# Keys and queries of an attention projected together, 512 columns at a time

## The chip, the cores and the metric

The kernel runs on one core of a Trainium2 chip. The metric is the device time of one execution in microseconds (us): the median of three runs of the kernel before is 1073.49 us (1072.52 to 1073.66). Five engines work side by side, each through its own instructions in a fixed order: TensorE (PE) multiplies matrices, and its weight loads are listed apart as PEld; VectorE (DVE), ScalarE (ACT) and GpSimd (POOL) work elementwise; SyncE (SP) only issues DMA transfers. ACT and POOL issue DMA transfers too.

## The reference

One layer of a hybrid decoder over 512 tokens with 16 meta tokens ahead of them: a first feed-forward network, a token-mixing part with two attention branches, and a second feed-forward network. The part that matters here is the mixing. Cut to it:

```
h   = rms_norm(x, g)
qkv = h @ w_in                       # 1024 inputs
fox: 8 heads of 64, q k v; log_f = log_sigmoid(h @ w_f + b)   # one forget value per token and head
     s = (rms(q) . rms(k)) / 8 + c[q] - c[k],  c = cumsum(log_f); causal softmax; times v
swa: 8 query heads, 2 key/value heads of 64, window 128, sinks, relative bias; softmax; times v
two gated branches, summed and projected
```

Each query and key head is normalised over its 64 values before the scores. Everything is float32 in and out.

## The kernel before

Every float32 product is made of three matmuls of a rounded format: both operands are split into a high and a low part, and high x high, high x low and low x high are summed in PSUM. Weights arrive by DMA as pieces of up to 128 x 1024 (raw, three buffers, issued by SP at line 252), ACT rounds them to wh (L133), and DVE subtracts to wl (L140). The helper piece() hands out the next split piece and keeps loads and splits a few pieces ahead.

Mixing is projected in chunks of 256 columns: for fox, two halves of four heads each with a chunk for v, k and q; for the sliding branch one of k and v and two of q. A chunk takes two pieces, each of four of the eight blocks of inputs, and goes over the tokens in tiles: tile 0 is the meta tokens, 16 rows, multiplied by a packed copy xm (two matmuls a block, tok_step at L1005 and L1006), then four tiles of 128 tokens with 24 matmuls of 256 columns each (prod, L301 to L304). tok_chunk makes two half-steps for each tile. After a tile of keys or queries, head_norm runs: ACT squares (L1057), DVE reduces per head (L1058) and scales (L1059), POOL raises to the power -1/2 (L351, rsq), ACT makes a scaled copy (L1072), DVE multiplies by the norm (L1079); the multiply is placed one tile later. When the last tile is through, finish transposes the heads on PE (L1159, L1167), ACT and DVE store the high and low parts (L134, L142).

The forget values become a table of biases. forget_sums transposes them on PE (L1195, L1197), copies and sums them along the tokens on DVE (L1201 to L1204), reorders them on POOL (L1207, L1208) and writes them to memory as cbd by SP (L1205, L1209). load_cb(p) reads them back, spread over all partitions, into a tile cb and a part of zA (L1235): by SP for the first pair of heads, by ACT for the next ones. mask_late(p) puts the causal mask in with an affine select on POOL (L1239). The scores of a pair need kH, kL, qH and, once they leave PSUM, cb.

Attention itself is written as units for each pair of heads, and while a unit's softmax runs, PE is given half-steps of later chunks as fills: a function weave mixes the two lists. Written order is not final: a scheduler with its own costs sets each engine's order when the kernel is built, and each engine then works through its list without overtaking, so that an instruction that waits holds all behind it on the same engine.

oA (the attention outputs) and zA (gates, and in part the biases) live in two tiles of a pool that stays through the mixing and the second feed-forward network. They are empty, but for the biases, while the first chunks are projected. The start of the mixing in code:

```
ka = qk_chunk(f0, "k", every, 1)
qa = qk_chunk(f0, "q", toks, 0)
va = v_chunk(f1)
run(ka[:-1] + qa[:LAG] + ka[-1:] + [forget_sums, lambda: load_cb(0)] + qa[LAG:-1]
    + va[:3] + [lambda: mask_late(0)] + qa[-1:] + va[3:5])
```

## Time and profile before

| | |
|---|---|
| median of three runs | 1073.49 us (1072.52 to 1073.66) |
| the profiled execution | 1073.59 us, span 1071.5 us, TensorE clock 0.999 |
| PE, PEld busy | 1060.0 us, 1028.2 us |
| DVE, ACT, POOL busy | 892.4 us, 664.7 us, 212.3 us |
| the mixing's projections and attention | about 361 to 607 us of the span |

The profile's page gives busy time by engine and the costliest groups of instructions. Other views of the same trace list waits (engine, output and line of the waiting instruction, what released it, total us, times, longest), groups of instructions by line and shape (count, busy us, mean ns of one, idle time before them and what ended it), and a timeline (start in us, duration in us, engine, line, operation, count of merged instructions, and in brackets idle time before it). Matmuls overlap, so the distance from one start to the next is what a matmul costs, not the duration.

### The profile page before, as it was taken

Reading aid. Unit: us, or ns where it says so; the run is one execution under the profiler, and the core shown is the slowest. Engines: PE = TensorE matmul, PEld = TensorE weight load, DVE = VectorE, ACT = ScalarE, POOL = GpSimd, SP = SyncE. Lnnn points to the kernel's source line nnn. Section 1 sums busy time; section 2 is a strip of 40 time slices with the busy share of each in tenths; the row PEclk is TensorE's granted clock in tenths of the full one; section 3 lists DMA queues with packets and bytes.
Section 4 is the critical chain, followed back from the end, with each engine's and each line's share of the span. In section 5 each row is a group of like instructions: output and inputs, shape, how many; then the busy total and the mean of one; then the engine's idle time right before and its main releaser. Section 6 shows DMA issues by size and latency. Waiting matters only on the chain.

```text
span 1071.5 us, 22307 instructions
## 1 busy us (share of the span) xinstructions
PE 1060.0 (99%) x8515; PEld 1028.2 (96%) x8515; DVE 892.4 (83%) x1732; ACT 664.7 (62%) x1270; POOL 212.3 (20%) x281
## 2 busy tenths in 40 slices
PE   9999999999999999999999999999999999999997
PEld 8999999999999999999877899999999999999997
DVE  7988878888889678889887999788988788977884
ACT  7667456656666466667757766455665466645663
POOL 3011111111124442332200110001122111221210
PEclk9999999999999999999999999999999999999999
DMA  8787777688776413313211873657688777887763
GB/s 279 198 224 162 189 193 196 152 216 219 176 180 178 124 65 123 87 52 89 73 59 57 241 196 99 210 184 213 155 203 196 181 185 194 180 179 196 163 123 90
DMA packets 112571, 173.58 MB, mean 162 GB/s; under 512 B 10880, under 2 KB 59264, under 8 KB 112208
## 3 DMA queue, kind: packets, MB, share of 16 engines
q1 hardware_dynamic: 74464, 122.72, 36.5%
q0 software_dynamic: 29040, 37.83, 22.9%
q10 hardware_dynamic: 8960, 11.60, 3.2%
q8 instruction: 67, 1.10, 0.4%
q14 instruction: 40, 0.33, 0.1%
HBM read 167.89 MB, written 6.32 MB: 163 GB/s over the span
## 4 chain that ended last, share of the span: by engine, by line
PE 50%; DVE 2%; ACT 1%; issue 0%; ACTq 0%; DVEq 0%
PE ps L301 9%; PE ps L304 8%; PE ps L302 8%; PE pt L301 8%; PE pt L302 7%; PE pt L304 7%; PE ps L1481 1%; DVE wl L140 0%; PE pt L1481 0%; PE ps L1960 0%; DVE pL L140 0%; ACT t L1216 0%; PE pt L1498 0%; ACT wh L133 0%; PE pt L1500 0%
## 5 line engine op out<-in xcount | busy, mean ns | idle before, releaser
L301 PE MATMUL ps<-x,wh 128*128 128x256 f32 (+2 forms) x768 | 219.8, 286 | 0.2
L302 PE MATMUL ps<-x,wh 128*128 128x256 f32 (+2 forms) x768 | 218.9, 285 | 0.5 <-DVE x L142 0.4
L304 PE MATMUL ps<-x,wl 128*128 128x256 f32 (+2 forms) x768 | 218.8, 285 | 0.0
L140 DVE TENSOR_TENSOR wl<-raw,wh 128x1024 fp32r<-128x1024 f32 (+3 forms) x125 | 150.1, 1201 | 38.4 <-ACT wh L133 37.5
L133 ACT CAST wh<-raw 128x1024 fp32r<-128x1024 f32 (+3 forms) x125 | 128.6, 1030 | 81.3 <-PE ps L302 46.7
L301 PEld LDWEIGHTS ps<-x,wh 128*128 128x128 f32 x768 | 144.7, 189 | 1.8 <-ACT hT L686 0.3
L302 PEld LDWEIGHTS ps<-x,wh 128*128 128x128 f32 x768 | 144.4, 188 | 1.4 <-DVE x L142 0.9
L304 PEld LDWEIGHTS ps<-x,wl 128*128 128x128 f32 x768 | 144.6, 188 | 0.9
L301 PE MATMUL pt<-x,wh 128*128 128x256 f32 (+2 forms) x424 | 125.3, 296 | 0.0
L304 PE MATMUL pt<-x,wl 128*128 128x256 f32 (+2 forms) x424 | 124.6, 294 | 0.0
L133 ACT CAST wh<-tc 128x1024 fp32r<-128x1024 f32 (+1 forms) x70 | 71.8, 1026 | 66.0 <-DVE tc L234 55.7
L302 PE MATMUL pt<-x,wh 128*128 128x256 f32 (+2 forms) x392 | 112.5, 287 | 0.0
L140 DVE TENSOR_TENSOR wl<-tc,wh 128x1024 fp32r<-128x1024 f32 (+1 forms) x70 | 83.5, 1192 | 33.4 <-ACT wh L133 33.2
L301 PE MATMUL ps<-acts,wh 128*128 128x264 f32 (+1 forms) x352 | 100.5, 286 | 0.1
L304 PE MATMUL ps<-acts,wl 128*128 128x264 f32 (+1 forms) x352 | 99.8, 284 | 0.0
L302 PE MATMUL ps<-acts,wh 128*128 128x264 f32 (+1 forms) x352 | 99.7, 283 | 0.0
L140 DVE TENSOR_TENSOR wl<-rawC,wh 128x1024 fp32r<-128x1024 f32 (+1 forms) x70 | 84.2, 1202 | 5.7 <-ACT wh L133 5.2
L133 ACT CAST wh<-rawC 128x1024 fp32r<-128x1024 f32 (+1 forms) x70 | 71.5, 1022 | 22.5 <-PE pt L302 16.6
L301 PEld LDWEIGHTS pt<-x,wh 128*128 128x128 f32 x424 | 80.0, 189 | 2.3 <-ACT wh L133 0.2
L304 PEld LDWEIGHTS pt<-x,wl 128*128 128x128 f32 x424 | 79.8, 188 | 2.1
L302 PEld LDWEIGHTS pt<-x,wh 128*128 128x128 f32 x392 | 73.7, 188 | 0.6
L301 PEld LDWEIGHTS ps<-acts,wh 128*128 128x128 f32 x352 | 66.4, 189 | 0.7 <-DVE h2T L918 0.3
(447 smaller groups left out, 3248.2 us busy)
## 6 DMA issues: line engine op xcount, KB each, us to landing
rawC<-in_w1i_dram SPq DMA_DIRECT2D x20, 512.0 KB, 4.5
raw<-in_w1i_dram SPq DMA_DIRECT2D x40, 256.0 KB, 4.5
raw<-in_w2i_dram SPq DMA_DIRECT2D x40, 256.0 KB, 3.4
rawC<-in_w2i_dram SPq DMA_DIRECT2D x20, 512.0 KB, 4.2
raw<-in_wm_dram SPq DMA_DIRECT2D x18, 512.0 KB, 4.2
raw<-in_wout_dram SPq DMA_DIRECT2D x16, 512.0 KB, 4.3
rawD<-in_w1i_dram SPq DMA_DIRECT2D x20, 256.0 KB, 4.6
raw<-in_w1i_dram POOLq DMA_DIRECT2D x20, 256.0 KB, 5.7
```

Of the source, the lines that this page charges most:

```text
L133: return A.copy(o, i)
L140: return V.tensor_tensor(out=o, in0=i, in1=h, op=ALU.subtract)
L301: PE.matmul(ps, sH, mH, start=first, stop=False, **more)
L302: PE.matmul(ps, sH, mL, start=False, stop=False, **more)
L304: shared["mm"] = PE.matmul(ps, sL, mH, start=False, stop=last, **more)
L1481: PE.transpose(ps[:, P * hh : P * hh + P], ts_[hh][:, c0 : c0 + P], ident)
```

## The change

The chunks of k and q of one fox half become one chunk of 512 columns (kq_chunk), and so do v and k of the sliding branch with the first four of its query heads (kvq_chunk). Such a chunk has four pieces of weights, each of two blocks of inputs by 512 columns, and all four stay until its last tile. The buffers wh and wl hold three pieces beside what the next chunk takes, so the first two pieces of a joined chunk go into home tiles: the places of the first half of zA and the second half of oA. For that, oA and zA (and the later tenants of their places) become two tiles each, behind a class Split. The meta tile is still projected 256 columns wide, since only keys (and values) need it.

The norms of the eight (or six) heads of a joined tile are made together: one square into sqacc, one reduce, one scalar step and one power of eight columns. Scaled queries wait for their transposes in the second half of zA. Finishing is cut into three steps: the keys of the first pair, its queries, and the second pair later, or in the sliding chunk the first key head, all queries, and the second key head. forget_sums and load_cb(0) come after thirteen of the joined chunk's eighteen steps. The later loads of h2T are cut to fit the split tile.

```diff
-    for c in (4, 2, 0, 5, 3, 1, 8, 6, 7):
-        for k in (0, 4):
-            pieces.append(("w", [(wm[c][:, k : k + 4, :], 4, 256)]))
...
+    for cuts in (((4, whole),), ((2, whole), (0, whole)), ((5, whole),), ((3, whole), (1, whole)), ((8, vals), (8, keys_), (6, whole)), ((7, whole),)):
+        nk = 4 if len(cuts) == 1 else 2
+        for k in range(0, KD, nk):
+            part = [(wm[c][:, k : k + nk, w], nk, w.stop - w.start) for c, w in cuts]
...
+            pieces.append(("w", part, k // 2 if nk == 2 and k < 4 else None))
...
+            elif pieces[c][0] == "w" and len(pieces[c]) > 2 and pieces[c][2] is not None:
+                home = kp.tile([P, 2, 1024], F32R, tag=("z0", "o1")[pieces[c][2]], name=nm("home"))
+                wh, wl = home[:, 0], home[:, 1]
...
-    oA = kp.tile([P, 2, 4, S], F32, tag="o", name="oA")
-    zA = kp.tile([P, KD, S], F32, tag="z", name="zA")
+    oA = Split("oA", ("o0", "o1"), [4, S])
+    zA = Split("zA", ("z0", "z1"), [4, S])
+    zA.get(1)
...
+    def wide_chunk(alloc, evac, ends):
+
+        w, box = [None] * 4, {}
+
+        def one(i, j):
+            if i == 0 and j == 0:
+                alloc()
+            if j == 0:
+                box[i] = psum()
+            width = 512 if i else 256
+            for q in (j,) if i else (2 * j, 2 * j + 1):
+                if i == 0:
+                    w[q] = piece()
+                for k in (2 * q, 2 * q + 1):
+                    tok_step(box[i], i, w, k, width)
+            if j == (3 if i else 1):
+                box[i] = evac(i, tok_result(box[i], i, width))
+                if i:
+                    box[i - 1]()
+
+        def end(f):
+            if box[NB] is not None:
+                box[NB]()
+                box[NB] = None
+            f()
+
+        return [lambda i=i, j=j: one(i, j) for i in range(NB + 1) for j in range(4 if i else 2)], [lambda f=f: end(f) for f in ends]
...
-        sq = new("hsq", [P, 256], F32, 3)
-        ss = mp.tile([P, 4], F32, tag="hss", name=nm("hss"), bufs=4)[:n, :nh]
+        sq = new("hsq", [P, 256], F32, 3) if nh <= 4 else sqacc
+        ss = mp.tile([P, 8], F32, tag="hss", name=nm("hss"), bufs=4)[:n, :nh]
...
+    def in_z(j):
+        return zA[:, 4 + (j - 1) // 2, 256 * ((j - 1) % 2) : 256 * ((j - 1) % 2) + 256].rearrange("p (h d) -> p h d", d=HD)
...
+    def kq_chunk(box):
+        ka, ko, kf = heads(box, "k", 1)
+        qa, qo, qf = heads(box, "q", 0, in_z)
...
+        def evac(i, ps):
+            if i == 0:
+                return head_norm(ps, 0, 4, ko(0))
+            return head_norm(ps, i, 8, [(o, par, 0, 4) for o, par in ko(i)] + [(qo(i)[0], None, 4, 8)])
+
+        return wide_chunk(alloc, evac, (lambda: kf([0]), lambda: qf([0]), lambda: [kf([1]), qf([1])]))
...
-    ka = qk_chunk(f0, "k", every, 1)
-    qa = qk_chunk(f0, "q", toks, 0)
+    kq0, ends0 = kq_chunk(f0)
     va = v_chunk(f1)
-    run(ka[:-1] + qa[:LAG] + ka[-1:] + [forget_sums, lambda: load_cb(0)] + qa[LAG:-1] + va[:3] + [lambda: mask_late(0)] + qa[-1:] + va[3:5])
+    run(kq0[:13] + [forget_sums, lambda: load_cb(0)] + kq0[13:] + va[:3] + ends0[:1] + va[3:4] + [lambda: mask_late(0)] + ends0[1:2] + va[4:5])
...
-        va[5:] + k1[:-1] + q1[:LAG] + k1[-1:] + q1[LAG:-1] + kv[:LAG] + q1[-1:],
-        kv[LAG:-1] + qb0[:LAG] + kv[-1:] + qb0[LAG:-1] + qb1[:2] + qb0[-1:] + qb1[2:4],
-        qb1[4:-1] + gates[:LAG] + qb1[-1:] + gates[LAG:],
+        va[5:7] + ends0[2:] + va[7:] + kq1 + kvq[:2] + ends1[:1] + kvq[2:LAG] + ends1[1:2],
+        kvq[LAG : LAG + 1] + ends1[2:] + kvq[LAG + 1 :] + qb1[:1] + ends2[:1] + qb1[1:2] + ends2[1:2] + qb1[2:4],
+        qb1[4:5] + ends2[2:] + qb1[5:-1] + gates[:LAG] + qb1[-1:] + gates[LAG:],
```

How the built order moves at three places. The first is POOL around the end of the first keys and queries, before the change. hss is a tile's norms, t the forget sums, cb and zA the bias tiles. In brackets is what an instruction waits for: DMAHW is the landing of a transfer.

```order
L1289 MEMSET t_5558 128x16 [waits DVE_49,PE_49]
L1207 COPY t_5343<-t_5343 8x128 [waits DVE_49]
L1207 COPY t_5343<-t_5343 8x128 x3
L1208 COPY t_5343<-t_5343 8x16
L351 TENSOR_TENSOR hss_5373<-hss_5373,nhalf 128x4 [waits DVE_49,Pool_49]
L351 TENSOR_TENSOR hss_5407<-hss_5407,nhalf 128x4 [waits DVE_49,Pool_49]
L1289 MEMSET t_5559 128x16 [waits DMAHW7_49,DMAHW0_49,Pool_49]
L1145 MEMSET qn_5815 128x256
L351 TENSOR_TENSOR hss_5441<-hss_5441,nhalf 128x4 [waits DVE_49]
L1239 AFFINE_SELECT zA<-zA 128x2x128 [waits DMAHW1_49]
L1239 AFFINE_SELECT cb_5356<-cb_5356 128x2x128 [waits DMAHW2_49]
```

And in the changed kernel (its L357 is the power, L1325 the select):

```order
L1375 MEMSET t_5415 128x16 [waits DVE_49,PE_49]
L1293 COPY t_5227<-t_5227 8x128 [waits DVE_49]
L1293 COPY t_5227<-t_5227 8x128 x3
L1294 COPY t_5227<-t_5227 8x16
L357 TENSOR_TENSOR hss_5249<-hss_5249,nhalf 128x8 [waits DVE_49]
L1375 MEMSET t_5416 128x16 [waits DMAHW6_49,DMAHW5_49,Pool_49]
L1325 AFFINE_SELECT zA_4880<-zA_4880 128x2x128 [waits DMAHW0_49]
L1325 AFFINE_SELECT cb_5240<-cb_5240 128x2x128 [waits DMAHW1_49]
L357 TENSOR_TENSOR hss_5285<-hss_5285,nhalf 128x8 [waits DVE_49]
```

The power of the last tile (hss_5441 before, hss_5285 now) stood ahead of the two selects and stands behind them now.

The second place is the same moment on SP and ACT. SP before the change:

```order
L1205 DMA cbd<-t_5343 4x528 [waits DMASW7_49,DMASW6_49,DMAHW0_49,DVE_49,DMAHW2_49,PE_49,Pool_49]
L1209 DMA cbd<-t_5343 4x528 [waits Pool_49]
L1235 DMA cb_5356<-cbd 128x800 [waits DMAHW7_49,DMAHW0_49]
L1235 DMA zA<-cbd 128x2x256
L252 DMA raw_5454<-in_wm_dram 128x1024 [waits DMAHW4_49,DVE_49]
```

Now SP has (L1291 and L1295 write cbd, L1321 loads it, L255 loads weights):

```order
L1291 DMA cbd<-t_5227 4x528 [waits DMASW6_49,DVE_49,DMASW7_49,PE_49,Pool_49]
L1295 DMA cbd<-t_5227 4x528 [waits Pool_49]
L255 DMA raw_5301<-in_wm_dram 128x2x256 [waits DMAHW2_49,DMAHW1_49,DVE_49]
L1321 DMA cb_5240<-cbd 128x800 [waits DMAHW6_49,DMAHW5_49]
L1321 DMA zA_4880<-cbd 128x2x256
L255 DMA raw_5301<-in_wm_dram 128x2x256 [waits DMAHW3_49]
```

The first half of a weight load, which waits for DVE, has come between the writes and the load of cb; the DVE instruction that it waits for is the wl of the second value piece.

On ACT the cast of that value piece is L133 on wh_5104. The changed kernel's ACT at this moment:

```order
L133 CAST home_5298<-raw_5097 128x1024 [waits DMAHW2_49,DMAHW1_49,PE_49]
L133 CAST home_5304<-raw_5108 128x1024 [waits DMAHW4_49,DMAHW3_49,PE_49]
L1321 DMA zA_4880<-cbd 128x2x256 [waits DMAHW6_49,DMAHW5_49,DMAHW0_49]
L133 CAST wh_5104<-raw_5087 128x1024 [waits PE_49]
L1116 ACTIVATE sqacc<-pt_5260 128x512 [waits DVE_49,PE_49]
```

It stands directly behind ACT's own load from cbd, which waits for both writes; the square of the last tile stands behind it. Before the change the casts of both value pieces stood ahead of that load.

The third place is DVE at the end of the second joined chunk, from the reduce of its last tile to the multiplies that its transposes need. Changed kernel:

```order
L1117 TENSOR_REDUCE hss_6061<-sqacc 128x8 [waits Activation_49]
L1118 TENSOR_SCALAR hss_6061<-hss_6061,r1sq 128x8 [waits DVE_49]
L1143 TENSOR_TENSOR zA_4880<-zA_4880,hss_5943 128x256 [waits Pool_49]
L1143 TENSOR_TENSOR qn_5768<-qn_5768,hss_5943 128x2x64
L1143 TENSOR_TENSOR qn_5769<-qn_5769,hss_5943 128x2x64
L1176 TENSOR_TENSOR oA_5618<-pt_6104,hsq_6114 64x256 [waits Activation_49]
L140 TENSOR_TENSOR wl_6118<-raw_6088,wh_6117 128x1024 [waits DMAHW6_49]
L1053 TENSOR_TENSOR hsq_6137<-ps_6083,hsq_6137 16x256 [waits Activation_49]
L142 SCALAR_TENSOR_TENSOR kL_5637<-pt_6162,gq,kH_5636 64x2x16 [waits Activation_49]
L1117 TENSOR_REDUCE hss_6143<-hsq_6142 16x2 [waits Activation_49]
L1118 TENSOR_SCALAR hss_6143<-hss_6143,r1sq 16x2 [waits DVE_49]
L1143 TENSOR_TENSOR zA_4880<-zA_4880,hss_6061 128x256 [waits Pool_49]
```

Before the change, the same stretch for the last tile of the second half's queries:

```order
L1058 TENSOR_REDUCE hss_6342<-hsq_6341 128x4 [waits Activation_49]
L1059 TENSOR_SCALAR hss_6342<-hss_6342,r1sq 128x4 [waits DVE_49]
L1079 TENSOR_TENSOR qn_6289<-qn_6289,hss_6291 128x256 [waits Pool_49]
L140 TENSOR_TENSOR wl_6373<-raw_6069,wh_6372 128x1024 [waits DMAHW3_49,PE_49,Activation_49]
L1112 TENSOR_TENSOR oA<-pt_6349,hsq_6359 64x256 [waits Activation_49]
L1022 TENSOR_TENSOR hsq_6401<-ps_6384,hsq_6401 16x256 [waits Activation_49]
L140 TENSOR_TENSOR pH_6417<-pt_6416,pH_6417 64x256 [waits Activation_49]
L140 TENSOR_TENSOR pL_6424<-ps_6422,pH_6423 128x384 [waits Activation_49]
L1058 TENSOR_REDUCE hss_6407<-hsq_6406 16x2 [waits Activation_49]
L1059 TENSOR_SCALAR hss_6407<-hss_6407,r1sq 16x2 [waits DVE_49]
L1079 TENSOR_TENSOR qn_6340<-qn_6340,hss_6342 128x256 [waits Pool_49]
```

There are three multiplies of the tile before where one stood, and the softmax's splits (pH, pL) have left the stretch.

More of the change, by code (lines that the diff above doesn't have):

```diff
@@ L386, in x_blocks, with rows_of, __init__, get @@
         return Blocks([x_tile()[:, : 2 * w].rearrange("p (k c) -> p k c", c=w) for _ in range(KD // 2)])
+    def rows_of(t, p):
+        return t.get(p) if isinstance(t, Split) else t[:, p]
+    class Split:
+        def __init__(self, name, tags, shape, dt=F32):
+            self.name, self.tags, self.shape, self.dt, self.tiles = name, tags, shape, dt, {}
+        def get(self, j):
+            if j not in self.tiles:
+                self.tiles[j] = kp.tile([P] + self.shape, self.dt, tag=self.tags[j], name=nm(self.name))
+            return self.tiles[j]
+        def __getitem__(self, at):
+            p, k, *c = at
+            if isinstance(k, slice):
+                j = k.start // 4
+                k = slice(k.start - 4 * j, k.stop - 4 * j)
+            else:
+                j, k = k // 4, k % 4
+            return self.get(j)[(p, k, *c)]
     class Halves:
@@ L864, in parts @@
             def parts(src, c, n):
-                h, l = (got[u // 2][:, p, c : c + n].rearrange("p a q -> p (a q)") for p in range(2))
+                h, l = (rows_of(got[u // 2], p)[:, c : c + n].rearrange("p a q -> p (a q)") for p in range(2))
                 hi(h, src)
@@ L904, in down @@
         th = ff.th
-        src = {name: tuple([t[:, p, c] for t in acts] for p in range(2)) for name, c in SLOT.items()}
+        src = {name: tuple([rows_of(t, p)[:, c] for t in acts] for p in range(2)) for name, c in SLOT.items()}
         put = {
@@ L1065, in head_norm @@
             a, b = src, by
+            if isinstance(o, tuple) and len(o) == 1:
+                todo.append((o[0], *todo[-1][1:]))
+                continue
             if isinstance(o, tuple):
-                o, par = o
-                a, b = (v.rearrange("p (a b) d -> p a b d", b=2)[:, :, par] for v in (src, by))
+                o, par, *of = o
+                a, b = (v[:, slice(*of)] if of else v for v in (src, by))
+                if par is not None:
+                    a, b = (v.rearrange("p (a b) d -> p a b d", b=2)[:, :, par] for v in (a, b))
                 kept = None
@@ L1124, in v_chunk, with heads @@
         return tok_chunk(alloc, range(NB + 1), lambda i, ps: v_evac(box["v"], i, ps))
-    def qk_chunk(box, tag, tiles, gcol):
+    def heads(box, tag, gcol, kept=None):
         off = M if tag == "q" else 0
@@ L1146, in evac, with finish @@
             if off or i == 0:
-                return head_norm(ps, i, 4, [qn[i][:n]])
+                return [qn[i][:n]]
             pairs = lambda j: qn[j].rearrange("p (a b) d -> p a b d", b=2)
-            return head_norm(ps, i, 4, [(pairs(i)[:, :, 0], 0), (pairs(NB + 1 - i)[:, :, 1], 1)])
-        def finish():
+            return [(pairs(i)[:, :, 0], 0), (pairs(NB + 1 - i)[:, :, 1], 1)]
+        def finish(prs=range(2)):
             g = gq[:, gcol : gcol + 1]
             dH, dL = box[tag]
-            for pr in range(2):
+            for pr in prs:
                 ps = psum()
@@ L1162, in finish @@
                 lo(dL[d], ps, dH[d], g)
-            if off:
+            if off or 0 not in prs:
                 return
@@ L1173, in finish, with q_chunk, alloc @@
                 lo(dL[d], src, dH[d], g[hb])
-        return tok_chunk(alloc, tiles, evac, finish)
+        return alloc, outs, finish
+    def in_z(j):
+        return zA[:, 4 + (j - 1) // 2, 256 * ((j - 1) % 2) : 256 * ((j - 1) % 2) + 256].rearrange("p (h d) -> p h d", d=HD)
+    def q_chunk(box, gcol):
+        alloc, outs, finish = heads(box, "q", gcol)
+        return tok_chunk(alloc, range(1, NB + 1), lambda i, ps: head_norm(ps, i, 4, outs(i)), finish)
+    def kq_chunk(box):
+        ka, ko, kf = heads(box, "k", 1)
+        qa, qo, qf = heads(box, "q", 0, in_z)
+        def alloc():
+            ka()
+            qa()
+        def evac(i, ps):
[3 more added lines that the diff above has]
+        return wide_chunk(alloc, evac, (lambda: kf([0]), lambda: qf([0]), lambda: [kf([1]), qf([1])]))
     def log_forget():
@@ L1727, in swa_out @@
     def swa_out(m):
-        return oA[:, m // 4, m % 4]
+        return oA.get(m // 4)[:, m % 4]
     def sliding(*ms):
@@ L1855 @@
     banks["turn"] = False
-    h2T = kp.tile([P, KD, S], F32, tag="z", name="h2T")
-    for k in (slice(0, 2), slice(2, KD)):
+    h2T = Split("h2T", ("z0", "z1"), [4, S])
+    for k in (slice(0, 2), slice(2, 4), slice(4, KD)):
         G.dma_start(h2T[:, k, : S // 2], h1d[:, k, : S // 2])
@@ L1891 @@
         if hf:
-            x2 = kp.tile([P, KD, S], F32, tag="o", name="x2")
+            x2 = Split("x2", ("o0", "o1"), [4, S])
             X2 = Halves(None, x2, S // 2)
@@ L1921, in acts_tile2 @@
         if i == 2:
-            t = kp.tile([P, KD, S], F32, tag="o", name=nm("acts2")).bitcast(F32R).rearrange("p k c -> p (k c)")
+            return Split("acts2", ("o0", "o1"), [7, S // 2], F32R)
         else:
```

64 lines of the change are left out of this document (35 added, 29 removed).

## The prediction

> **What bounds the kernel now.** I read the page first, then the waits, and then the timelines of single engines at the place that the change rewrites. The page:
>
> ```profile
> span 1071.5 us, 22307 instructions
> PE 1060.0 (99%) x8515; PEld 1028.2 (96%) x8515; DVE 892.4 (83%) x1732; ACT 664.7 (62%) x1270; POOL 212.3 (20%) x281
> ```
>
> TensorE (PE) is busy for 99% of the span. So the time falls only if PE gets less to do or waits less, and it rises by every wait that PE does not have today. VectorE (DVE), at 83%, is the engine that PE waits for most. The waits of PE's weight loads between 361 and 600 us, where all edited code runs (columns: engine, output, line, what it waited for; total us, times, longest):
>
> ```profile
> PEld pt L1373 <- DVE pL L140: 2.4, 5, 1.0
> PEld ps L1159 <- DVE qn L1079: 1.0, 3, 0.6
> PEld ps L302 <- DVE wl L140: 0.4, 1, 0.4
> ```
>
> The second row is the transposes that finish heads, waiting for norms; the third is weights not split in time. There is little waiting to win: the rows of this stage come to about 6 us, and much of that belongs to softmax (the first row).
>
> **PE's own work.** The order of PE has 576 matmuls of 256 columns in the chunks concerned replaced by 288 of 512. Three rows of a run of 256-column matmuls (start, duration as modelled) and the two ends of a run of 512-column ones:
>
> ```profile
> 439.80 0.28 PE L304 MATMUL pt<-wh,x 128*128 128x256 f32 x1
> 439.91 0.28 PE L301 MATMUL pt<-wh,x 128*128 128x256 f32 x1
> ...
> 440.86 0.28 PE L304 MATMUL pt<-wh,x 128*128 128x256 f32 x1
> 593.25 0.39 PE L301 MATMUL pt<-x,wh 128*128 128x512 f32 x1
> ...
> 594.87 0.40 PE L302 MATMUL pt<-x,wh 128*128 128x512 f32 x1
> ```
>
> Nine steps in 1.06 us are 118 ns each; seven steps in 1.62 us are 231 ns. Two narrow passes cost 236 ns and one wide pass 231, so a pair saves 5 ns, and 288 pairs save **1.4 us** (bounds 1 to 2, by rounding of the starts). The Trainium skill ("TensorE: Matmul & The Clock Gate", "Back-to-back issue gap") gives a sustained spacing of about 131 ns at 512 columns, against 216 ns for isolated ones. By it 288 pairs would save 288 x (236 - 131) = 30 us. This trace shows 231 ns in an unbroken run, so the rule does not hold here; it stands as a rival with a token chance.
>
> **Work taken off the other engines.** Rows of the stage by shape (count | busy us, mean ns | idle before):
>
> ```profile
> L140 DVE TENSOR_TENSOR wl<-raw,wh 128x1024 fp32r<-128x1024 f32 x19 | 23.3, 1224 | 2.6 <-ACT wh L133 2.5
> L1058 DVE TENSOR_REDUCE hss<-hsq 128x4 f32<-128x256 f32 x24 | 9.9, 413 | 6.0 <-ACT hsq L1057 6.0
> L1079 DVE TENSOR_TENSOR qn<-qn,hss 128x256 f32<-128x256 f32 x16 | 6.7, 418 | 2.3 <-POOL hss L351 2.3
> L1079 DVE TENSOR_TENSOR qn<-qn,hss 128x128 f32<-128x128 f32 x24 | 6.2, 286 | 0.3 <-POOL hss L351 0.3
> L1059 DVE TENSOR_SCALAR hss<-hss,r1sq 128x4 f32<-128x4 f32 x24 | 5.5, 228 | 0.7
> L1057 ACT ACTIVATE hsq<-ps 128x256 f32<-128x256 f32 x14 | 5.4, 386 | 8.8 <-PE ps L304 7.7 <-DMA cbd<-t 1.1
> L133 ACT CAST wh<-raw 128x1024 fp32r<-128x1024 f32 x19 | 20.0, 1054 | 9.4 <-PE pt L304 5.7 <-PE ps L304 2.0 <-issue 1.7
> L351 POOL TENSOR_TENSOR hss<-hss,nhalf 128x4 f32<-128x4 f32 x24 | 25.9, 1082 | 41.9 <-DVE hss L1059 41.9
> L351 POOL TENSOR_TENSOR hss<-hss,nhalf 128x2 f32<-128x2 f32 x4 | 2.8, 709 | 5.3 <-DVE hss L1059 5.3
> ```
>
> Twelve tensor_scalars go (12 x 0.228 = 2.7 us) and twelve reduces are merged into longer ones; a merged pair saves its fixed part, some 0.14 us if the step from 128 to 256 columns in the multiplies (0.286 to 0.418) is a guide. That is 4.4 us of DVE and, by the same reasoning, 1.9 us of ACT, all beside PE. It shortens only those waits of PE that end on DVE. I credit **-1 us**, bounds 0 and -3: softmax's own chain, which ends most of them, is untouched.
>
> In return the last step of a joined chunk has a longer chain. Two columns of the power cost 0.709 us on POOL and four 1.082, so 0.187 a column: eight are estimated at 1.83. The Trainium skill ("GPSIMD Engine Reference", "3.1 Elementwise — side-by-side cycle accounting") gives about 2.6 cycles an element for tensor_tensor, by which four columns more would be almost free, and the sum 0.75 us lower. The two rows, with 0.187 us a column, speak against it for this power.
>
> **The end of the first joined chunk: the main term.** Write T for the end of its last matmul. Today the place looks like this, engine by engine (behind them, us from issue to landing: of cb and of two weight loads at this place, and of all such weight loads):
>
> ```profile
> 395.21 0.27 PE L1195 MATMUL pt<-ident,lf 128*8 128x128 f32 x1
> 395.67 0.36 PE L301 MATMUL pt<-wh,x 128*128 128x256 f32 x1
> 396.96 0.15 DVE L1201 COPY t<-pt 8x16 f32<-8x16 f32 x1
> 401.21 0.23 POOL L1208 COPY t<-t 8x16 f32<-8x16 f32 x1
> 401.46 0.59 SPq L1209 DMA_DIRECT2D cbd<-t  x1
> 403.23 0.34 SPq L1235 DMA_DIRECT2D cb<-cbd  x1
> 403.62 0.43 SPq L1235 DMA_DIRECT2D zA<-cbd  x1
> 404.15 3.86 SPq L252 DMA_DIRECT2D raw<-in_wm_dram  x2
> 403.23 0.42 ACTq L1235 DMA_DIRECT2D zA<-cbd  x1
> 403.75 0.39 ACT L1057 ACTIVATE hsq<-ps 128x256 f32<-128x256 f32 x1 [1.06 <-DMA cbd<-t]
> 404.94 1.11 POOL L351 TENSOR_TENSOR hss<-hss,nhalf 128x4 f32<-128x4 f32 x1 [1.25 <-DVE hss L1059]
> 407.78 0.42 POOL L1239 TENSOR_SCALAR_AFFINE_SELECT zA<-zA 128x256 f32<-128x256 f32 x1 [1.74 <-DMA zA<-cbd]
> 408.16 0.41 POOL L1239 TENSOR_SCALAR_AFFINE_SELECT cb<-cb 128x256 f32<-128x256 f32 x1
> cb<-cbd SPq DMA_DIRECT2D x1, 400.0 KB, 3.9
> raw<-in_wm_dram SPq DMA_DIRECT2D x2, 512.0 KB, 6.4
> raw<-in_wm_dram SPq DMA_DIRECT2D x18, 512.0 KB, 4.2
> 406.41 0.60 PE L1159 MATMUL pt<-ident,qn 128*128 128x128 f32 x4
> ```
>
> Three readings. The load of cb is issued 8.0 us after the forget transposes begin (395.21 to 403.23). ACT's Square at 403.75 sat idle for 1.06 us behind ACT's own load, which waits for the write to cbd: a load that waits holds the engine that issues it. POOL's select at 407.78 waited 1.74 us for a landing, but by then the last power (404.94) had run, so PE's transposes at 406.41 lost nothing.
>
> After the change each of the three queues has the dangerous thing in front. On POOL both selects stand before the last tile's power. On SP the first half of a weight load stands before cb's load, and it waits for a raw buffer that comes free when wl of the second value piece is made. On ACT the cast of that very piece stands behind ACT's load of zA. So the chain runs through all three:
>
> - The forget transposes begin 30 wide matmuls plus their own 0.46 us (395.21 to 395.67) before T: 30 x 0.231 + 0.46 = 7.4. Eight us later is T+0.6; DVE started its copies at 396.96, some 1 us late behind keys, and that may be gone. cbd has landed, and ACT is let go, between T-0.4 and T+0.6.
> - ACT's issue 0.42, cast 1.05, DVE's wl 1.22: T+2.3 to T+3.3.
> - SP issues the half piece (0.34) and then cb: T+2.6 to T+3.6. It lands in 3.9 us on an empty queue; behind 256 KB about 1 us later (estimate: a weight load of 512 KB lands in 4.2 us, and two that share the queues here in 6.4, so half of one costs its follower 1.1). T+6.5 to T+8.5.
> - POOL's select 0.41, the power of eight columns 1.83; DVE's multiply of the queries 0.42, the add of the meta partial in between (0.41), the multiply of half the keys 0.29: 3.36 together. The first key transposes can start at T+9.9 to T+11.9.
> - PE reaches them, unhindered, after 33 narrow matmuls and two transposes: 33 x 0.118 + 0.2 = T+4.1.
>
> The stall is 5.8 to 7.8 us; I take the middle, **+6.8**. PE also stops for that wl itself on the way, at T+1.7; that is inside the 6.8, not beside it. What this place loses today, 0.4 us for weights (the third wait row) and 0.2 beside it, goes: **-0.6**. Behind it the chain from transposes to scores (keys, then queries, 0.7 us an operation on each engine) is about as long as PE's 3.2 us of work there: **+0.2**.
>
> What is queued behind the waiting instructions: the next weights' second half on SP, behind zA, lands about T+9 to T+10 and its split is then just ahead of the keys' on DVE. It costs nothing unless it lands later than that; it is the upper case below.
>
> **The end of the second joined chunk.** There PE has 16 narrow meta matmuls, nine for the values of a pair and two transposes, some 3.5 us at 118 ns with the changes between them, before the transposes of the last tile. DVE has to do: reduce of 512 (0.7, scaled), tensor_scalar 0.23, the previous tile's three multiplies (0.42 + 2 x 0.286), an output add 0.42, a weight split 1.22, the meta add, reduce and scalar (about 1), and then its multiplies (0.42 + 0.286); with Square ahead of it some 6 us. The stall is 2 to 2.8 where the second wait row has 1.0 today: **+1.5** net. The third joined chunk has 7 us of other matmuls there and needs none.
>
> **The start.** All four pieces of the joined weights are needed in its first step, where two were. The last split is made within half a microsecond of PE's need: **+0.3**, bounds 0 and 0.6. Values, softmax and everything after 607 us keep their work; the splitting of tiles there moves loads by one issue and costs nothing while the transfers are ahead by microseconds.
>
> **Sum.** -1.4 - 1.0 + 6.8 - 0.6 + 0.2 + 1.5 + 0.3 = **+5.8 us**. The profiled execution took 1073.59, within 0.1 us of the median of 1073.49, so the forecast is **1079.3 us**. Around it the bounds of the terms give 1077.5 to 1081.5.
>
> **The rivals.**
>
> 1. *Relief wins.* If the forget chain ends so early that cb lands by T+1.5, the last power runs on time: the select is over when its input is there. Place and price: the 6.8 and 0.2 go, and a VectorE with 4.4 us less to do takes the 3 us of its bound off the old waits: -1.4 - 0.6 + 1.5 + 0.3 - 3 = -3.2, 1070.4. For it: DVE would be freer when the forget rows come. Against it: eight us from transpose to load issue and 3.9 to landing, 12 in all, against the 9 that there are (7.4 + 1.5). Chance 0.09.
> 2. *POOL alone waits.* The raw buffer comes free in time, SP goes straight on, and cb lands at T+3.5 to T+4.5; the power starts then, and the transposes wait 3.3 instead of 6.8 (4.0 + 3.4 - 4.1). 1075.8. For it: only a few tenths separate the cast from the landing. Against: the order has that cast behind the waiting load. Chance 0.19.
> 3. *A longer chain only.* The selects do not hold the power. Square 0.65 and reduce 0.7 (scaled from 0.386 and 0.413), scalar 0.23, power 1.83, multiplies and add 1.12: T+4.5 against 4.1, a stall of 0.4 for the 6.8; the sum is -0.6, 1073.0. This is also the case that the change does nothing that can be measured. Against: POOL works in its order. Chance 0.11.
> 4. *The queue backs up further.* The next weights land after T+11, hold keys' split on DVE, and the second chunk's wait is the full 2.8: 1082 to 1083. Chance 0.14.
> 5. *Wide passes overlap*, which would be worth 30 us. The 231 ns speak against it. Chance 0.01.
>
> **How the numbers follow.** The forecast keeps 0.46. A difference under 0.2%, 2.1 us, cannot be told from none. Faster takes rivals 1 and 5: 0.10. Same takes rival 3 and the low edge of rival 2: 0.13. Slower has the rest, 0.77. The range from 1073.5 to 1083 holds the forecast, rivals 2 and 4 and the upper half of rival 3, about 8 in 10.
>
> **What would show it.** In the profile after: on PE a gap of 5 to 8 us, in one or two pieces, between the end of the first joined chunk and its first transposes, put down to wl and then to the norm; POOL idle before the selects, ended by the landing of cb; the power of eight columns after them at 1.8 us; SP's load of cb 2 us or more after the write to cbd has landed. Then about 2.5 us at the second chunk's transposes, and 230 ns between wide matmuls. It is wrong if POOL's power runs before cb lands, or if cb's load goes out as soon as cbd has landed.

## The result and the profile after

The changed kernel takes 1080.74 us (median; 1080.08 to 1081.96) against 1073.32 (1072.12 to 1074.03) for the kernel before: a ratio of 1.0072, 95% interval 1.0059 to 1.0085. It is slower by 7.4 us, forecast were 5.8. The profiled execution took 1080.36 us. Its page, the engines' row:

```profile
span 1078.6 us, 21677 instructions
PE 1061.4 (98%) x8227; PEld 1015.9 (94%) x8227; DVE 890.5 (83%) x1708; ACT 663.8 (62%) x1258; POOL 208.6 (19%) x271
```

PE has 288 matmuls fewer and is busy 1.4 us longer; DVE has lost 1.9 us of work and ACT 0.9. Where the time came in shows when three marks are laid side by side in the timelines: the first matmul of the changed chunks, the first scores, and the first matmul of the output projection. Before:

```profile
375.96 0.36 PE L1005 MATMUL pt<-wh,xm 128*128 128x256 f32 x1
411.13 0.44 PE L1299 MATMUL pt<-kH,qH 64*128 64x400 f32 x1
599.47 0.39 PE L302 MATMUL pt<-oLs,wh 128*128 128x512 f32 x1
```

After:

```profile
376.82 0.36 PE L1036 MATMUL pt<-home,xm 128*128 128x256 f32 x1
416.65 0.45 PE L1385 MATMUL pt<-kH,qH 64*128 64x400 f32 x1
608.37 0.39 PE L308 MATMUL pt<-oLs,wh 128*128 128x512 f32 x1
```

From the first mark to the scores it was 35.2 us and is 39.8 (+4.7); from there to the output projection it was 188.3 and is 191.7 (+3.4). The 0.9 us ahead of the first mark lies before the joined chunks; that mark stands anywhere between 376.2 and 376.9 in the changed kernels run here. The end gives 1.8 back, for the last output writes landed sooner in this profile. Together that is the 7.1 us by which the span grew.

The waits of PE between 361 and 610 us (engine, output, line, what it waited for: total us, times, longest) begin with two single ones that the kernel before does not have:

```profile
PE ps L1223 <- DVE qn L1143: 4.1, 1, 4.1
PE pt L1223 <- DVE zA L1143: 3.4, 1, 3.4
```

**The first place**, by engine, at the end of the first joined chunk. T, the end of its last matmul, is 401.61; the matmul at 405.94 is PE's last ahead of the wait:

```profile
398.82 0.59 SPq L1295 DMA_DIRECT2D cbd<-t  x1
400.12 0.38 SPq L255 DMA_DIRECT2D raw<-in_wm_dram  x1
400.64 0.36 SPq L1321 DMA_DIRECT2D cb<-cbd  x1
401.06 0.43 SPq L1321 DMA_DIRECT2D zA<-cbd  x1
400.68 0.40 ACTq L1321 DMA_DIRECT2D zA<-cbd  x1
401.12 1.05 ACT L133 CAST wh<-raw 128x1024 fp32r<-128x1024 f32 x1 [1.03 <-DMA cbd<-t]
400.71 0.11 POOL L1375 MEMSET t<- 128x16 f32 x1 [0.27 <-DMA cbd<-t]
406.67 0.42 POOL L1325 TENSOR_SCALAR_AFFINE_SELECT zA<-zA 128x256 f32<-128x256 f32 x1 [5.84 <-DMA zA<-cbd]
407.41 1.64 POOL L357 TENSOR_TENSOR hss<-hss,nhalf 128x8 f32<-128x8 f32 x1
404.06 0.23 DVE L1118 TENSOR_SCALAR hss<-hss,r1sq 128x8 f32<-128x8 f32 x1
409.08 0.62 DVE L1143 TENSOR_TENSOR zA<-zA,hss 128x256 f32<-128x256 f32 x1 [4.07 <-POOL hss L357]
405.94 0.28 PE L308 MATMUL pt<-wl,x 128*128 128x256 f32 x1
410.28 1.12 PE L1223 MATMUL ps<-ident,qn 128*128 128x128 f32 x4 [4.07 <-DVE qn L1143]
```

cbd lands at about 400.65: it frees ACT, POOL and SP at once, and the load of cb goes out at 400.64, T-1.0, not T+2.6 or later. The wl of the second value piece, which was to hold SP by the prediction and by the description of the built order ahead of it, is made from the cast of 401.12, after the load. So the half weight load at 400.12 did not wait for it; I had given that load the wrong buffer. It went out when the first of two earlier splits on DVE, into a home tile, was through (398.87 plus 1.22 us). The rest is as forecast: the select stands ahead of the power and waits 5.84 us for a bias tile, while the power's input was there at 404.3. That tile is the part of zA for the second pair of heads: the select waits for the semaphore of the load that ACT issued at 400.68, and that load landed at 406.60. The first pair's cb, by which the prediction timed the select, had landed at 405.98. From 406.67 the chain takes 3.6 us to the transposes (forecast 3.4 from the landing).

**The clock.** The table of windows (us; PE, PEld, DVE, ACT and POOL busy with their counts; granted clock of PE; DMA share; GB/s) around both places:

```profile
401.60:406.00 4.40, 4.33 (x36) 4.12 (x34) 2.78 (x6) 2.31 (x6) 0.00 (x0) 1.00 0.99 226
406.00:410.20 4.20, 0.22 (x2) 0.01 (x1) 1.12 (x4) 0.76 (x1) 3.51 (x11) 0.77 1.06 378
410.20:415.10 4.90, 4.82 (x23) 4.82 (x24) 3.48 (x8) 3.00 (x7) 1.48 (x4) 0.50 0.53 143
415.10:420.00 4.90, 4.90 (x48) 4.65 (x47) 3.80 (x13) 1.75 (x5) 0.23 (x1) 1.00 0.07 24
473.20:476.50 3.30, 3.30 (x17) 2.46 (x17) 2.14 (x5) 0.76 (x3) 0.00 (x0) 0.50 0.00 0
```

After the first wait PE works 4.9 us at half clock (23 matmul records where the next 4.9 us hold 48). In windows of 0.1 us the clock is 1.00 or 0.50: it is 0.50 for 6.8 us from 408.2, which is inside the first wait, and for 3.4 us from 473.1, which is 1.4 us after the second. The forecast had nothing of this. The Trainium skill ("TensorE: Matmul & The Clock Gate", "Part 1: The HAM clock gate") says that a free-running activity window of about 3.4 us sets TensorE to half rate after an idle window, and back after a busy one. The half rate agrees, and so do the lengths at half clock, one and two times 3.4 us. That the whole window must be idle does not: in experiment 9 a wait of 2.14 us was followed by 3.4 us at 0.50, in experiment 11 one of 2.68.

**The second place**, DVE and PE at the end of the second joined chunk, whose last matmul ends at 464.3:

```profile
464.91 1.21 DVE L140 TENSOR_TENSOR wl<-raw,wh 128x1024 fp32r<-128x1024 f32 x1
466.05 0.67 DVE L1117 TENSOR_REDUCE hss<-sqacc 128x8 f32<-128x512 f32 x1
467.07 1.74 POOL L357 TENSOR_TENSOR hss<-hss,nhalf 128x8 f32<-128x8 f32 x1 [2.14 <-DVE hss L1118]
468.73 1.23 DVE L140 TENSOR_TENSOR wl<-raw,wh 128x1024 fp32r<-128x1024 f32 x1
471.08 0.22 DVE L1118 TENSOR_SCALAR hss<-hss,r1sq 16x2 f32<-16x2 f32 x1
471.22 0.41 DVE L1143 TENSOR_TENSOR zA<-zA,hss 128x256 f32<-128x256 f32 x1
471.68 0.33 PE L1223 MATMUL pt<-ident,zA 128*128 128x128 f32 x1 [3.43 <-DVE zA L1143]
```

The power is through at 468.8; its multiplies come 2.4 us later, for they are written behind the next chunk's meta tile, down to its scalar step (471.08).

### The profile page after: what moved, and what is told of

It reads as the page before. It is cut to its first block, busy times and chain, and to the rows that moved or that the text cites. A ratio compares the mean times of both kernels' runs of the same rounds, so it can differ in the third digit from the quotient of the medians.

```text
span 1078.6 us, 21677 instructions
## 1 busy us (share of the span) xinstructions
PE 1061.4 (98%) x8227; PEld 1015.9 (94%) x8227; DVE 890.5 (83%) x1708; ACT 663.8 (62%) x1258; POOL 208.6 (19%) x271
## 4 chain that ended last, share of the span: by engine, by line
PE 48%; DVE 3%; ACT 1%; issue 0%; DVEq 0%; ACTq 0%
PE ps L307 8%; PE ps L310 8%; PE ps L308 8%; PE pt L307 7%; PE pt L308 7%; PE pt L310 7%; ACT t L1302 1%; DVE wl L140 1%; DVE pL L140 0%; PE ps L1568 0%; PE ps L2049 0%; DVE t L1305 0%; PE pt L1568 0%; ACT wh L133 0%; PE pt L1585 0%
## 5 line engine op out<-in xcount | busy, mean ns | idle before, releaser
L140 DVE TENSOR_TENSOR wl<-raw,wh 128x1024 fp32r<-128x1024 f32 (+3 forms) x119 | 142.7, 1200 | 46.8 <-ACT wh L133 45.9
L133 ACT CAST wh<-raw 128x1024 fp32r<-128x1024 f32 (+3 forms) x119 | 122.2, 1029 | 93.3 <-PE ps L308 49.9
L133 ACT CAST wh<-tc 128x1024 fp32r<-128x1024 f32 (+1 forms) x70 | 71.8, 1025 | 66.0 <-DVE tc L237 57.6
L133 ACT CAST wh<-rawC 128x1024 fp32r<-128x1024 f32 (+1 forms) x70 | 71.6, 1023 | 22.0 <-PE pt L308 15.9
```

Of the source, the lines that this page charges most:

```text
L133: return A.copy(o, i)
L140: return V.tensor_tensor(out=o, in0=i, in1=h, op=ALU.subtract)
```

## The experiments

Each ratio is against the kernel before on the same chip. The first group starts from the changed kernel.

**1. The selects behind the last power.** The selects of the first two pairs of heads are ordered behind the power of the joined chunk's last tile:

```diff
+        if not p:
+            shared["last"] = shared["pow"]
+        with after(shared["last"]):
+            mask_late(p)
```

> Only POOL's order is edited: the causal selects of the first two pairs are queued behind the power of the joined chunk's last tile; every transfer, and its issue, stays as it is. Theory A (POOL waits for the landing of the bias tiles, and the last norm waits behind it; the slow clock after the stall is its consequence): the power runs at about 404.4 us, the first key transposes wait about 1 us instead of 4.1, the granted clock stays at 1.0, and 3.1 + 2.4 us go: about 1075.2 us. Theory B (the rival that the prediction's sum rests on: SP and ACT are held by the second value piece, and the weights of the value chunk arrive late): the order of POOL alone gives back at most the select's 0.4 us and PE still waits 3 us or more: above 1079 us.

1080.27 us (1077.74 to 1081.24), ratio 1.0066 [1.0053, 1.0079]. Its timeline at the first place:

```profile
404.04 1.74 POOL L357 TENSOR_TENSOR hss<-hss,nhalf 128x8 f32<-128x8 f32 x1 [3.54 <-DVE hss L1118]
406.82 0.66 PE L1223 MATMUL ps<-ident,qn 128*128 128x128 f32 x4 [0.94 <-DVE qn L1143]
408.83 1.05 ACT L133 CAST wh<-raw 128x1024 fp32r<-128x1024 f32 x1 [4.18 <-DMA raw<-in_wm_dram]
410.32 0.69 ACT L134 ACTIVATE kH<-ps,gq 128x512 fp32r<-128x512 f32 x1
412.16 0.45 PE L1385 MATMUL pt<-kH,qH 64*128 64x400 f32 x1 [1.12 <-ACT qH L134]
```

The mechanism was right: the power runs as soon as its input is there, and PE waits 0.94 us, not 4.07. The scores come 4.2 us sooner after the chunk's start; they would come sooner still, but ACT's cast waits 4.18 us for late weights ahead of kH, and PE then 1.12 for qH. But the total does not move. Two of its windows (columns as above) show where the gain goes:

```profile
412.00:418.00 6.00, 5.39 (x31) 4.47 (x32) 5.62 (x20) 2.55 (x8) 2.12 (x7) 0.72 0.30 87
470.30:476.00 5.70, 5.66 (x25) 4.59 (x26) 3.09 (x8) 2.02 (x4) 0.95 (x1) 0.52 0.16 63
```

The clock did not stay at 1.0, as Theory A had it: it fell at 414.2, behind waits of only 0.94 and 1.12 us, and stayed at 0.50 for 3.4 us. From the first scores to the first transposes of the softmax it takes 7.2 us, where the changed kernel takes 4.6, so 2.7 of the 4.2 us are gone there. The remainder goes at the second place, where the wait grew from 3.4 to 4.3 us and the half clock from 3.4 to 6.8. The forecast of a lower total missed.

**2. The last multiplies at once.** In the second joined chunk they are written ahead of the next chunk's meta tile:

```diff
-        va[5:7] + ends0[2:] + va[7:] + kq1 + kvq[:2] + ends1[:1] + ...
+        va[5:7] + ends0[2:] + va[7:] + kq1 + flush1 + kvq[:2] + ends1[:1] + ...
```

> Only the second joined chunk is edited: the multiplies of its last tile are written ahead of the next chunk's meta tile, so that on DVE they no longer stand behind that tile's scalar step, a weight split and an output add. Theory A (the wait of 3.4 us at 471.7 us is a matter of DVE's order, tied to the meta tile of the next chunk): the wait falls to about 1.2 us, the slow clock behind it goes too, and 2.3 + 2.0 us are saved: about 1076.4 us. Theory B (DVE simply has too much work there, or the power of eight columns is what is late): the wait stays above 2.5 us, and the time above 1079.5 us.

1079.7 us (1078.94 to 1080.07), ratio 1.006 [1.0048, 1.0073]. The wait at the second place fell to 1.2 us; the first stayed at 4.4. So the written order made most of the second wait, and the low clock behind it is gone too. But the forecast of 1076.4 us missed: the medians are 1 us apart, and the two ratios' intervals overlap widely. From the first scores to the output projection it takes 1.4 us less than in the changed kernel; where the remainder of the 4.3 us went is not settled.

**3. Both.**

> Both edits together: the selects behind the last power, and the last multiplies ahead of the next meta tile. If both waits are matters of queue order and add up, 5.5 + 4.3 us go: about 1071 us, 2 us under the kernel before, which is what the joined chunks then bring by themselves (1.4 us of pitch, and shorter waits). If the waits share a cause, or the gain is taken back by later waits, it stays at 1074 us or above.

1078.01 us (1076.22 to 1078.73), ratio 1.0046 [1.0032, 1.006]. Two executions kept PE's clock at 1.0 and took 1076.22 and 1076.54; three ran at a mean of 0.996 or 0.997 and took 1078.01, 1078.52 and 1078.73. The same program thus differs by 2.0 us (means) with the clock. The two gains do not add up to the forecast of 1071 us; the rival, 1074 us or above, is what came.

**4. Work in the gap.** 34 matmuls that nobody reads fill the first wait, so that PE is not idle there:

```diff
+        for _ in range(34):
+            PE.matmul(ps[:, :256], xH[:, 0, M : M + P], xH[:, 0, M : M + 256], start=True, stop=True)
```

> The changed kernel with 34 matmuls of 256 columns added on PE (4.0 us at 118 ns), whose result nobody reads, placed ahead of the first key transposes, where PE sits idle for 4.1 us. Nothing else waits for them. Theory A (the clock of 0.50 from 410 to 415 us is the consequence of PE's idling): PE does 4 us more, the granted clock stays at 1.0 there, and the time falls by about 2 us, to some 1078.5 us. Theory B (the slow clock comes from something else, or the added work is not covered): the clock still drops, or the time rises by up to 4 us.

1081.0 us (1079.8 to 1081.71), ratio 1.0072 [1.006, 1.0085]. The window of the first place, columns as above:

```profile
402.00:418.00 16.00, 14.73 (x128) 14.07 (x127) 10.40 (x28) 6.55 (x17) 5.00 (x15) 1.00 0.67 202
```

The clock stays at 1.00, and from the transposes to the first scores it takes 4.97 us (410.00 to 414.97), where the changed kernel takes 6.37 (410.28 to 416.65). So the idling itself made the clock fall. Its fall costs at least 1.4 us on the path. The stretch of the filled kernel also holds five more matmuls of values and two more transposes, about 0.7 us at their distances, so the price is some 2.1 us by estimate; 4.9 us at half clock lose 2.45. The total, forecast at 1078.5, is again unchanged: the second wait grew to 3.7 us, and its clock from 470.3 to 476 us was 0.53.

**5. The forget sums sooner**, on top of 1: forget_sums and load_cb(0) after nine steps of the first chunk.

```diff
-    run(kq0[:13] + [forget_sums, lambda: load_cb(0)] + kq0[13:] + ...
+    run(kq0[:9] + [forget_sums, lambda: load_cb(0)] + kq0[9:] + ...
```

> The selects behind the last power, and the forget sums with the first load of the biases written after nine steps of the first joined chunk instead of thirteen, 24 wide matmuls or 5.5 us earlier. ACT's load of zA, which held the cast of the second value piece, and the four bias loads then run before the chunk ends, and the next chunk's weights no longer share the queues with them. Theory A (what is left at the first place is the bias traffic: ACT held by its load, and the next weights late behind 1.3 MB of biases, so that their cast stands ahead of the keys' high part): the wait at the first transposes falls from 1.1 to about 0.5 us, the waits of 2.5 us at the first scores fall under 1 us, and the first scores are reached 2.5 us earlier than with the selects moved alone; the second place still waits 4.5 us with a slow clock after it: about 1077 us. Theory B (the longer norm chain and the weights themselves are late): both waits stay within 0.5 us of what they were, above 1079.5 us.

1076.46 us (1074.97 to 1077.64), ratio 1.0031 [1.0021, 1.0041]. Nothing waits at the first scores any more; they come 34.5 us after the first mark, where the kernel before needs 35.2. The second wait is 4.3 us. The first wait stayed at 1.1 us and did not fall to 0.5, and the scores come 1.1 us sooner than in experiment 1, not 2.5; but the clock stays at 1.00 at the first place, and the total is near Theory A's 1077. With the loads of the bias away from those of the weights, the gain of 1 is kept.

**6. Experiment 5 with experiment 2.**

> The same, and the last multiplies of the second joined chunk ahead of the next meta tile. With the selects and the multiplies moved, the time was 1076.2 to 1076.5 us in the executions whose clock stayed at 1.0 and 1078.0 to 1078.7 us where it fell to 0.996. If the 2.5 us at the first scores go, and with them the cause of the clock's drop: the clock is 1.0 in every execution and the time about 1073.7 us, level with the kernel before. If the clock still drops in some: 1075 to 1076 us.

1073.69 us (1073.26 to 1074.77), ratio 1.0008 [0.9999, 1.0017]. That is the decisive run: with the three orders mended and the wide projection and joined norms left as they are, the loss of 7.4 us is down to 0.9 by ratio, and the clock is 0.999 or above in every execution.

**7 to 9. Cover and order for the two waits that are left** (1.2 us each). 7 adds a step of the sliding chunk ahead of the second chunk's finish; 8 also multiplies the keys ahead of the queries, since they are transposed first; 9 also puts twelve more matmuls ahead of the first finish:

```diff
-        ... + kq1 + flush1 + kvq[:2] + ends1[:1] + kvq[2:LAG] + ends1[1:2],
+        ... + kq1 + flush1 + kvq[:LAG] + ends1[:1] + kvq[LAG : LAG + 1] + ends1[1:2],
-                for o, a, b in reversed(todo):
+                for o, a, b in reversed(todo) if nh <= 4 else todo[-2::-1] + todo[-1:]:
-    ... + va[:3] + ends0[:1] + va[3:4] + [selects] + ends0[1:2] + va[4:5])
+    ... + va[:4] + ends0[:1] + [selects] + ends0[1:2] + va[4:5])
```

> The same, and the first finishing step of the second joined chunk one step of the next chunk later, so that 1.4 us more of matmuls stand ahead of the transposes that still wait 1.45 us for the longer norm chain. If this cover is free, the wait goes and the time falls by 1.4 us to about 1072.3 us, under the kernel before by 1 us. If the step is merely moved (the scores of the next pair come later, and the softmax behind them waits instead), it stays at the time of the run before, within 0.5 us.

> On top of the run with the cover: of a joined tile DVE multiplies the keys first and the queries last; before, the queries' 0.42 us came first although the transposes that PE waits for are those of the keys. If the two waits that are left (1.35 and 1.48 us) are the end of the norm's chain, each falls by about 0.4 us and the time by 0.8, to about 1072.3 us. If they hang on something else, nothing changes.

> As with the keys first, and at the first place the transposes come half a tile of values later, behind 12 more matmuls of 256 columns (1.4 us). If PE's idle time there is only the norm's chain, the wait of about 0.9 us is covered and the time is about 1071.4 us, 1.2 us or more under the kernel before. If the first scores then come later by as much, because the keys' high and low parts are the path, it stays within 0.3 us of the run with the keys first.

7: 1073.14 us (1072.41 to 1075.42), ratio 1.0003 [0.9994, 1.0012]. 8: 1072.64 (1072.08 to 1078.37), 1.0007 [0.9995, 1.0019]. 9: 1072.62 (1071.64 to 1076.93), 1.0002 [0.9992, 1.0012]. None can be told from the kernel before. In 7 the second wait stayed, at 1.3 us; probably the cover also delays the work that DVE has to do. In 8 the two waits fell by a quarter of a microsecond each (to 0.9 and 1.1), not by 0.4. In 9 the first wait went, the second grew to 2.1, and the clock fell behind it:

```profile
464.90:468.20 3.30, 3.22 (x13) 3.07 (x14) 2.96 (x7) 1.80 (x5) 0.43 (x1) 0.50 0.15 24
```

So cover at these places was not enough by itself.

**10. The norms apart**, on top of 7: two squares, reduces, scalar steps and powers of four columns for each tile of the fox chunks; the matmuls stay 512 wide.

```diff
-            return head_norm(ps, i, 8, [(o, par, 0, 4) for o, par in ko(i)] + [(qo(i)[0], None, 4, 8)])
+            scales = head_norm(ps, i, 4, ko(i)), head_norm(ps[:, 256:], i, 4, qo(i))
+            return lambda: run(scales)
```

> On top of the run with the cover: the joined norms of keys and queries are made apart again, four heads each; the matmuls stay 512 wide. It undoes the one part of the change that takes work off DVE and ACT (8 reduces, 8 scalar steps, 8 squares more; powers of 1.08 us in place of 1.74). Theory A (the prediction's credit: relief of DVE and ACT shortens PE's waits by 1 us): the time rises by 0.5 us or more, to 1073.7 us or above. Theory B (relief is hidden, and the longer chain of the joined norm is what PE sees): the waits at the two ends fall by about 0.5 us each and the time by 0.5 to 1 us, to 1072.5 us or below.

1072.47 us (1071.32 to 1074.76), ratio 0.9993 [0.9985, 1.0002], against 1.0003 with joined norms (7); the two intervals overlap, so the time alone does not decide. The waits do: the one at the first place is gone, and of the second place's two steps this is left:

```profile
463.83 0.66 PE L1223 MATMUL pt<-ident,qn 128*128 128x128 f32 x4 [1.03 <-DVE qn L1143]
469.23 0.45 PE L1386 MATMUL pt<-kH,qH 64*128 64x400 f32 x1 [0.43 <-ACT kH L134]
```

In 7 the two waits were 1.1 and 1.3 us. So the work that joined norms save is not what PE waits for; the longer chain of the joined norm is a part of it.

**11. The changed kernel with only the norms apart**, to see how much of the loss the joined norm makes without the other edits.

> The changed kernel with only the norms of keys and of queries made apart again (two squares, two reduces, two scalar steps and two powers of four columns a tile); projections stay 512 wide, the order stays the changed one. Theory A (order of the queues): the selects still stand ahead of the last powers on POOL and the last multiplies of the second joined chunk still stand behind the next chunk's meta step, so the stalls of about 4 us at the first place and 3 to 4 at the second remain, with the low clock behind them: 1079 to 1081. Theory B (the longer chain of the joined norm makes the stalls): they shrink to under 2 us each, 1074 to 1077. A change of DVE's load by 4 us has no effect of its own in either.

1078.48 us (1076.94 to 1079.58), ratio 1.0052 [1.0038, 1.0066]. Its first select and both its large waits:

```profile
405.23 0.42 POOL L1326 TENSOR_SCALAR_AFFINE_SELECT zA<-zA 128x256 f32<-128x256 f32 x1 [4.04 <-DMA zA<-cbd]
408.03 0.55 PE L1223 MATMUL ps<-ident,qn 128*128 128x128 f32 x3 [2.68 <-DVE qn L1143]
469.43 0.66 PE L1223 MATMUL ps<-ident,qn 128*128 128x128 f32 x4 [3.49 <-DVE qn L1143]
```

It lies between the two expectations, nearer to that of the queues: the select still waits for its load ahead of the powers, PE still waits 2.68 and 3.49 us, and the clock is still lower behind both (0.66 and 0.63). In this order the joined norm makes about 2 of the 7.4 us (1.0072 against 1.0052, with intervals that just overlap). The orders mended with the norm left joined (experiment 6) gave back 6.9 by ratio; the two shares overlap and do not add up.

**12. One more step of cover behind the second finish**, on top of 10:

```diff
-        ... + kvq[:LAG] + ends1[:1] + kvq[LAG : LAG + 1] + ends1[1:2],
-        ends1[2:] + kvq[LAG + 1 :] + ...
+        ... + kvq[:LAG] + ends1[:1] + kvq[LAG : LAG + 1] + ends1[1:2] + kvq[LAG + 1 : LAG + 2],
+        ends1[2:] + kvq[LAG + 2 :] + ...
```

> The last version (norms apart, forget sums early, multiplies written at once, finish one step later) with one more step of the sliding chunk between the second and the third finish of the second joined chunk. If the 1.3 us that PE still waits there for split keys is a lack of cover, it goes: 1071.3 to 1071.8. If the wait only moves to the next transposes, no change: 1072.3 to 1072.7. If the later finish holds softmax, 1073 or more.

1070.8 us (1070.39 to 1071.66), ratio 0.9979 [0.9969, 0.9988]: faster than both kernels, and half a microsecond below what was expected. From its page:

```profile
PE 1058.0 (99%) x8227; PEld 1012.8 (95%) x8227; DVE 892.6 (84%) x1724; ACT 663.9 (62%) x1266; POOL 211.0 (20%) x279
```

And the three marks in its timeline:

```profile
376.28 0.36 PE L1036 MATMUL pt<-home,xm 128*128 128x256 f32 x1
409.44 0.45 PE L1386 MATMUL pt<-kH,qH 64*128 64x400 f32 x1
598.10 0.39 PE L308 MATMUL pt<-oLs,wh 128*128 128x512 f32 x1
```

PE works 2.0 us less than before, and no wait at either place is above 0.4 us. From the first mark to the output projection it is 221.8 us, before 223.5, in the changed kernel 231.6. This is the wide projection without its stalls: 1.7 us saved, and the forecast's 5 ns a pair would make 1.4 of them. The kernel before was not run with its own orders mended in this way, so a part of the gain may not belong to the wide projection. Why the wait of 1.03 at the second place vanished with a step that comes behind it is not settled; the scheduler moved its neighbours too.

## Why the prediction was right, and where not

The direction, the size (+5.8 forecast, +7.4 measured) and both places were right; the way in which the first stall arises was half right, and several errors offset each other.

- **Pitch, -1.4.** Right: the last tile's 24 wide matmuls in the timeline after, first and last:

```profile
396.05 0.40 PE L307 MATMUL pt<-home,x 128*128 128x512 f32 x1
...
401.38 0.39 PE L310 MATMUL pt<-wh,x 128*128 128x512 f32 x1
```

23 steps of 0.232 us. Wide passes start no closer here than the forecast had them, and rival 5 falls.
- **Relief, -1.** Wrong. DVE's busy time fell by 1.9 us and not 4.4. The durations were sized well (a merged reduce takes 0.68 us in place of twice 0.413, so 0.15 less, where 0.14 was taken), but on DVE an instruction starts before its predecessor's record ends (471.08 plus 0.22, then 471.22), so that a sum of durations, which did fall by 4.4 us over reduces and scalar steps, is more than the time that comes free. Little came of it on PE: the listed waits beside the two new ones add up to 1.7 us, before to 2.1. The step that failed is "I credit -1 us": the norm's longer chain ends PE's waits, as experiments 10 and 11 show. The power itself was sized well, as the groups of 361 to 545 us in the profile after show (count | busy us, mean ns | idle before):

```profile
L357 POOL TENSOR_TENSOR hss<-hss,nhalf 128x8 f32<-128x8 f32 x8 | 13.8, 1721 | 15.6 <-DVE hss L1118 15.6
L1117 DVE TENSOR_REDUCE hss<-sqacc 128x8 f32<-128x512 f32 x8 | 5.4, 680 | 7.4 <-ACT sqacc L1116 7.4
```

1.72 us, against an estimate of 1.83 and 1.08 for four columns. By the rule of the Trainium skill ("GPSIMD Engine Reference", "3.1 Elementwise — side-by-side cycle accounting") four more columns would be almost free; these rows disagree.

- **The first place, +6.8.** What held was that POOL's selects wait for a load and hold the power, and that ACT is held 1.03 us by its own load. What failed is the third bullet, "SP issues the half piece (0.34) and then cb: T+2.6 to T+3.6": SP issued at T-1.0, by the prediction's own test the sign that this step is wrong. Rival 2, given 0.19, had the mechanism. cb landed within its T+3.5 to T+4.5, at T+4.4; but the select waited for the second pair's zA, at T+5.0, and the stall of 3.3 us is 4.2 in PE's starts. The first bullet was off as well: cbd landed at T-1.0, before its earliest T-0.4. The loads landed late, by the trace's list of issues from 398 to 403 us:

```profile
cb<-cbd SPq DMA_DIRECT2D x1, 400.0 KB, 5.3
zA<-cbd ACTq DMA_DIRECT2D x1, 256.0 KB, 5.9
```

where cb took 3.9 before and ACT's zA 4.5. The DMA engines were full from 401.6 to 410 (shares 0.99 and 1.06 above), with weights queued beside four bias loads. That the sharing made them late is argued from these rows; no run isolated it, though experiment 5 moved the bias loads away and kept its gain. The slow clock, 1.4 to 2.1 us by experiment 4, stood in for part of the stall that did not come. To the first scores the terms of this place and a third of the pitch gave +5.9 and the trace has +4.7.
- **The second place, +1.5.** Right in cause, too small. The multiplies came 6.9 us after the chunk's last matmul, not 6, because a weight split (464.91) stood ahead of the reduce too; the wait was 3.4 us for 2 to 2.8, and 3.4 us at half clock followed. From the scores to the output projection the trace has +3.4 with two thirds of the pitch in it, so +4.3 without.
- **The start, +0.3.** No such wait is in PE's list; the term is zero.

Relief was credited and did not come, the first stall was shorter and the second longer, and the clock was left out. From the forecast of +5.8 to the 7.1 us of the spans: 1.0 of relief not had, 1.2 less to the scores, 2.8 more behind them, 0.3 less at the start, and 0.9 given back outside of the joined chunks (+0.9 ahead of them, -1.8 at the end), which leaves 0.1 of rounding. That the sum came this close is partly luck.

## What to carry to other kernels

When several small operations are joined, the operations saved count only where the slow engine waits for their sum, while the longer last chain is paid wherever that engine has little to do in between. Before such an edit, look on each queue at what stands ahead of the last step of the chain: a select that waits for a load, bias loads beside weight loads and another chunk's start cost more here (6.9 us given back with the norm left joined) than the joined norm (about 2). And mend all such places together: against the changed kernel's 1.0072 the selects alone gave 1.0066, the multiplies alone 1.006, both 1.0046, and with the bias loads moved as well 1.0008.

## What the hardware showed that was not expected

A single wait of 2 us or more of an otherwise full PE came with a stretch at half clock, and this clock took two values only, 1.00 and 0.50. Over the two places in all profiles, the waits of 2.1 to 3.5 us (2.14, 2.68, 3.43 and 3.49) each came with 3.4 us at 0.50, and those of 3.7 to 4.4 us (3.74, 4.07, 4.28, 4.32 and 4.39) each with 6.8. Matmuls of 256 columns then start 0.21 us apart (411.41 to 411.63) and not 0.118. Filling the wait with unread matmuls keeps the clock at 1.00; the fall costs 1.4 to 2.1 us at the first place.

Waits of about 1 us are the uncertain case. In experiment 1 waits of 0.94 and 1.12 us were followed by 3.4 us at 0.50; in the profiles of 3 and 8 such waits were not. The clock also makes one program's executions differ: 2.0 us in experiment 3, and in experiment 8 two executions at clock 0.995 and 0.996 took 1078.37 and 1077.36 where the others, at 0.998 or above, took 1072.08 to 1073.81. Those two were not profiled, so which waits made their clock fall stays open. In experiment 12, without such waits, all executions lie within 1.3 us.
